# A two-layer diffusion trunk: second layer's output projection by token tiles, begun inside attention, with shared SBUF places and single PSUM banks

## Chip, cores and metric

One core of one Trainium2 chip runs the whole program. The metric is device time in microseconds of one execution, as the median of several runs. All arithmetic is 32-bit. TensorE (PE) multiplies; VectorE (DVE), ScalarE (ACT) and GpSimd (POOL) do the rest; SyncE (SP) issues most transfers, POOL's queue a few.

## The reference, cut to what matters

Two layers over 1024 latent tokens and 256 context tokens of width 1024. The first layer (grouped attention beside a gated scan, then a convolutional FFN) isn't touched. The second layer reads both and returns the latent tokens alone:

```python
def odd_mixer(h_lat, h_ctx, w_qkv, w_out, rpb, with_ctx_out):
    ...
    # per grid row: 8 x 16 neighbourhood plus all context keys in one softmax, 16 heads of 64
    o = lax.map(row_block, (jnp.arange(rows), q.transpose(1, 0, 2, 3, 4)))
    y_lat = o.transpose(1, 0, 2, 3, 4).reshape(B_, L, C_W) @ w_out
```

After the mixer: y is RMS-normed, multiplied by a gate, and added to the residual x2, which gives x3. Then x3 is RMS-normed, scaled and shifted, and goes through the FFN:

```python
def conv_ffn(h, w_up, conv_w, conv_b, w_down):
    u = h @ w_up
    u = lax.conv_general_dilated(u, conv_w[:, None, :], ...) + conv_b
    a, g = jnp.split(u, 2, axis=-1)
    return (jax.nn.silu(g) * a) @ w_down
```

with another gated residual behind it.

## The kernel before

**Exact products.** A 32-bit operand is split into a high part (a rounding copy, called `hi`, `h` or `..h`) and a low part (a subtraction). A product is three matmuls: high by high, high by low, low by high (L115 is the one line that records them all). A split costs one copy on ACT and one subtraction, on DVE or POOL.

**Stages of the second layer.** `odd_values` (L1766 on) norms x2, transposes it into `xh`, `xl` (channels by tokens, one tile of 40 KB per partition each) and projects the values, which go to DRAM (`vcd`). `odd_attention` computes the rest in one loop. `odd_out` is a stage of its own. `last` runs the FFN, `ffn(1, ...)`.

**Attention.** `project()` is a generator that yields after every three matmuls of the query and key projection; the loop over 128 jobs (16 heads, 8 query tiles) calls it through `step`, 46 times ahead and then two or three times per iteration. An iteration holds the scores of job i on PE, their minimum and bias on DVE (L2003), the exponential of job i-1 on ACT (L2009), the transposes of job i-3 with a copy on ACT and a subtraction on DVE (L2034, L2035), the values of job i-5, and the division of job i-1, a `tensor_scalar` on POOL over 640 columns (L2015). `finish` adds the halves of a head's output and stores them to DRAM (`ocd`, by pairs of heads, tokens grouped by 8-column strips). Projected queries and keys live in a ring of four places (`c_qa`, `c_qb`, `c_k`). Projection uses two PSUM banks (`g_ps`), transposes three, scores two, values one. The generator runs dry at job 110; the last 17 jobs and the drain run without it.

**Output projection.** `odd_out` loads `ocd` by halves of the tokens (two halves of 512, `a_oT`), splits it (L2209, L2210), and `out_proj` loads and splits the weights for each half of the columns and of the tokens anew (`granule`, L133, L135). For four token tiles at a time `y_half` squares and copies a PSUM bank out (L312, L313); `y_finish` loads x2 (L331), applies rstd and gate (L322), adds (L325) and stores x3 to DRAM (L326).

**FFN.** `ffn_norm` loads all rows of x3, norms each in SBUF (L1121 square, `rstd` with a power on POOL at L123, L1125 scale), transposes in groups of four tiles (L1145), applies scale and shift (L1157) and forms sums for a product scheme of seven half-size products instead of eight: operands `B11`, `B21` (first 512 tokens), `T1` to `T4`, `B22`, each split. `sums()` yields between these. `ffn_up` runs 22 feature tiles of 128 channels; `first(j)`, the product of A11 and B11, stands ahead of its tile. For j = 0 the loop draws `sums()` between products, and `add(u2, ...)`, which frees a bank for the S3 by T3 product, stands behind the T3 sums. `ffn_down` is behind the last tile.

**Order.** Within these stages `in_order` fixes the order of PE, ACT, DVE and POOL to the order of the program text; each engine's queue is served in order. SP's transfers are placed by the scheduler and then also issued in order, each behind the wait of the one ahead of it. A tile with one buffer is written again only when its last reader is done, and a pool that opens on memory of a closed pool waits tile by tile.

Of the kernel before, what the change touches and what calls it, by code (L numbers as in the profile page):

```python
# [20 lines left out]
P = 128  # L21
# [21 lines left out]
BLOCKS = ((0, 512), (512, 512), (1024, 256))  # L43

# [17 lines left out]
class Trunk:  # L62
# [54 lines left out]
    def rstd(self, ms, n, p=P):  # L117

        nc = self.nc
        e = self.small.tile([P, 16], F32, name="rs_e")  # L120
        r = self.small.tile([P, 16], F32, name="rs_r")
        nc.vector.tensor_scalar(e[:p, :n], ms, EPS, None, op0=OP.add)  # L122
        nc.gpsimd.tensor_tensor(out=r[:p, :n], in0=e[:p, :n], in1=self.mhalf[:p, :n], op=OP.pow)  # L123
        return r[:p, :n]

    def granule(self, src, a, b, lo="pool"):
# [9 lines left out]
        return hi, lo_t  # L136

# [204 lines left out]
    def qk_norm_rope(self, ps, nh, t, w, sp, dup):  # L342
# [7 lines left out]
        ms = self.small.tile([P, 16], F32, name="qk_ms")  # L350
# [850 lines left out]

    def ffn_up(self, l, src, ctx, x_src, x_dst, hp, pp, tp, es, beside):
# [58 lines left out]
        def first_out(j):  # L1261
            if j < FK:
                st["p1"] = half("f_p1")
                nc.scalar.copy(st["p1"], st["G", j][:, :512])
# [25 lines left out]
        with self.in_order(*self.compute), ExitStack() as loads:  # L1290
# [18 lines left out]
            sp = self.pool(es, f"fu{l}", 2)  # L1309
            cw = sp.tile([P, 48, 4], F32, name="cw", bufs=1)[:, 0:44, :]  # L1310
            nc.sync.dma_start(cw, a["convT"][l])
# [6 lines left out]
            first_out(0)  # L1318

            down = iter(())  # L1320
            for j in range(FK):
# [11 lines left out]
                product(st["G", j][:, :512], ("A12",), "B21", False, True)  # L1333
# [16 lines left out]
                split(n, "A11")  # L1350
# [4 lines left out]
                product(Z, ("S1",), "T1", True, False)  # L1355
                if j == 0:
                    next(sums)
                u2 = st["u2"] = half("f_u2")
                add(u2, V[:, 512:], st["p1"])
# [26 lines left out]
                first(n)  # L1386
# [379 lines left out]
    def odd_values(self, nx, xh, xl, gp, tp, sp):  # L1766
# [22 lines left out]
        def modulate(n0, tiles, s):  # L1789
            n = P * len(tiles)  # L1790
            for k in range(KT):
                pt = tp.tile([P, 512], F32, name="n_pt", tag="tp")
                for i, t in enumerate(tiles):
# [3 lines left out]
                nc.vector.tensor_copy(xh[:, k, n0:n0 + n], t[:, :n])  # L1797
                nc.vector.tensor_tensor(out=xl[:, k, n0:n0 + n], in0=t[:, :n], in1=xh[:, k, n0:n0 + n].bitcast(F32),
                                        op=OP.subtract)
# [13 lines left out]
        def products(tiles):  # L1813

            for c in range(2):
                for t in tiles:
                    ps = gp.tile([P, 512], F32, name="g_ps")
                    for k in range(KT):
                        wh, wl = (w[:, 512 * (k % 2):512 * (k % 2) + 512] for w in W[4 * c + k // 2])
                        xhk, xlk = xh[:, k, t * P:(t + 1) * P], xl[:, k, t * P:(t + 1) * P]  # L1820
# [58 lines left out]
    def odd_attention(self, xh, xl, gp, tp, pp, sp):  # L1879
# [9 lines left out]
        for i in range(4):  # L1889
            q1 = sp.tile([P, SEQ], F32R, name=f"c_qa{i}", bufs=1)  # L1890
            q2 = sp.tile([P, SEQ], F32R, name=f"c_qb{i}", bufs=1)
            kk = sp.tile([P, NTOK], F32R, name=f"c_k{i}", bufs=1)
            nc.gpsimd.memset(q2[64:128].bitcast(F32), 0.0)
            ring.append((q1, q2, kk))
# [30 lines left out]
        def evacuate(c, j, n0, n, ps, s):  # L1925

            q1, q2, kk = ring[(2 * c + s) % 4]
# [6 lines left out]
            else:  # L1934
                nc.scalar.copy(kk[0:64, cs], ps[r, :n])
                nc.vector.tensor_tensor(out=kk[64:128, cs], in0=ps[r, :n], in1=kk[0:64, cs].bitcast(F32), op=OP.subtract)

        def project():
# [3 lines left out]
            for c in range(KT):  # L1942
                for j, blocks in ((0, BLOCKS[:2]), (1, (BLOCKS[0], BLOCKS[2], BLOCKS[1]))):
                    for n0, n in blocks:
                        ps = gp.tile([P, 512], F32, name="g_ps")
                        for k in range(KT):
                            m = 4 * c + 2 * j + k // 4
                            wh, wl = (w[:, (k % 4) * P:(k % 4) * P + P] for w in wts[m])
                            xhk, xlk = xh[:, k, n0:n0 + n], xl[:, k, n0:n0 + n]
# [11 lines left out]
            yield KT  # L1961

# [12 lines left out]
        def value_load(h, ts):  # L1975
            for t in ts:
                v = sp.tile([P, 2, P], F32R, name="c_v", bufs=8)
# [6 lines left out]
        def scores(h, b, ql):  # L1984
            g = 2 * b + ql
            q1, q2, kk = ring[h % 4]
# [10 lines left out]
            for o, k0, w in parts:  # L1997
                for i, q in enumerate((q1, q2)):
                    self.mm(ps[:, o:o + w], q[:, g * P:(g + 1) * P], kk[:, k0:k0 + w], i == 0, i == 1)
# [55 lines left out]
        def finish(h, b, pv):  # L2055
            tu = sp.tile([P, 256], F32, name="c_o", bufs=1)
            o, t = tu[0:64], tu[64:128]
            nc.scalar.copy(t, pv[64:128, :256])
            nc.vector.tensor_tensor(out=o, in0=pv[0:64, :256], in1=t, op=OP.add)
            r = 64 * (h % 2)  # L2060
            nc.sync.dma_start(self.ocd[h // 2][r:r + 64, 256 * b:256 * b + 256], o)

        fill = project()
        at = 0
# [6 lines left out]
        with self.in_order(*self.compute):  # L2071
            load(0)
            load(1)
            for m in range(3):
                prepare(m)
            bias_load(0)
            value_load(0, (8, 0, 2))
            bias(0)
            step(46)
# [5 lines left out]
            for i in range(N + 6):  # L2085
                if i < N:
# [26 lines left out]
                step(1)  # L2113


    def run(self, stages=5):
        for f in (self.even_in, self.even_out, self.middle, self.odd_out, self.last)[:stages]:
# [55 lines left out]
    def odd_in(self, nx, early):  # L2173
        pool = self.pool
        with ExitStack() as es:
            hp = pool(es, "h1")
            xh = hp.tile([P, KT, NTOK], F32R, name="xh")
            xl = hp.tile([P, KT, NTOK], F32R, name="xl")
            with ExitStack() as e2:
                gp = pool(e2, "g_psum", 4, space=PSUM)  # L2180
                tp = pool(e2, "t_psum", 3, space=PSUM)
                sp = pool(e2, "n1", 2)
                self.weights(e2, 3, 8)
                self.odd_values(nx, xh, xl, gp, tp, sp)
            early.close()
            with ExitStack() as e2:
                sp = pool(e2, "na", 2)
                self.weights(e2, 2, 2)
                gp = pool(e2, "g_psum", 2, space=PSUM)
# [133 lines left out]
```

## Time and profile before

| quantity | value |
|---|---|
| median of three runs | 3415.87 us (3415.09 to 3416.26) |
| the profiled execution | 3415.23 us, its span 3413.3 us |
| granted TensorE clock, mean over the span | 0.957 |
| busy: PE, DVE, ACT, POOL | 91%, 60%, 44%, 45% |
| attention's loop with projection beside it | about 2165 to 2523 us |
| attention without it | 2523 to 2575 us |
| output projection | 2575 to 2683 us |
| norm of the FFN and its first feature tile | 2683 to 2773 us |
| FFN up, feature tiles at 19.05 us each | from there |

A slice of the page's second part is a fortieth of the span, and its digits are busy tenths. In a timeline row, the bracket at the end is how long the engine had stood idle and what released it. In a row of a group, the part behind the bar is the busy sum and the mean of one in ns, then the idle time ahead of it. In the chain of waits, a row is start, duration and what was waited for.

### The profile page before, as it was taken

How to read it: one execution, taken by the hardware profiler on the slowest of the kernel's cores; microseconds unless marked ns; L12 is line 12 of the kernel's file. 1: busy time of each engine (PE TensorE's matmuls, PEld its weight loads, DVE VectorE, ACT ScalarE, POOL GpSimd, SP SyncE). 2: the span in 40 equal slices, each digit the busy share in tenths (PEclk: the TensorE clock that was granted, in tenths of full speed). 3: DMA queues.
4: the chain of work that ended last, by engine and by line, in shares of the span. 5: the costliest groups of instructions: out<-in, count | busy, mean ns of one | idle time of the engine just before them, and what ended most of it. 6: DMA issues, size and time to landing. Idle time of an engine off the chain costs nothing.

```text
span 3413.3 us, 48746 instructions
## 1 busy us (share of the span) xinstructions
PE 3113.9 (91%) x18364; PEld 2567.7 (75%) x18364; DVE 2059.1 (60%) x3413; ACT 1487.1 (44%) x2619; POOL 1524.3 (45%) x1147
## 2 busy tenths in 40 slices
PE   5899998869998699999999989999997679999997
PEld 2776776658887488888878768898986468888785
DVE  3625666657775754545477863576775565555778
ACT  3223222256664543434344442566664344343443
POOL 1310111187774466666610111677771167777201
PEclk7999999979999799999999999999998799999998
DMA  7533333221112212212285772222216412222856
GB/s 233 161 100 130 129 119 115 101 90 38 50 44 73 95 68 68 71 63 73 75 299 194 255 237 110 69 61 65 63 45 186 139 53 90 75 91 75 272 186 214
DMA packets 203947, 399.24 MB, mean 117 GB/s; under 512 B 23216, under 2 KB 85168, under 8 KB 203712
## 3 DMA queue, kind: packets, MB, share of 16 engines
q1 hardware_dynamic: 194656, 364.15, 32.7%
q0 software_dynamic: 9056, 31.99, 2.4%
q8 instruction: 144, 2.36, 0.3%
q14 instruction: 91, 0.75, 0.1%
HBM read 322.11 MB, written 74.34 MB: 116 GB/s over the span
## 4 chain that ended last, share of the span: by engine, by line
PE 74%; DVE 10%; DMA 4%; ACT 4%; issue 4%; POOL 2%; SPq 1%; POOLq 0%; ACTq 0%; DVEq 0%
PE g_ps L115 20%; PE u_g L115 13%; PE d_ps L115 10%; PE u_v L115 10%; PE u_pc L115 4%; PE a_pv L115 2%; PE c_pv L115 2%; PE c_s L115 2%; PE a_pt L930 2%; PE c_pt L2032 2%; PE mod_ps L115 1%; DVE a_pl L932 1%; PE a_s L115 1%; ACT a_ph L931 1%; DMA y_x<-x2d 1%
## 5 line engine op out<-in xcount | busy, mean ns | idle before, releaser
L123 POOL TENSOR_TENSOR rs_r<-rs_e,mhalf 128x1 f32<-128x1 f32 (+3 forms) x106 | 81.1, 765 | 1006.7 <-DVE rs_e L122 1006.5
L115 PE MATMUL d_ps<-d_Bh,d_Ah 128*128 128x512 f32 x704 | 276.9, 393 | 9.5 <-ACT d_Bh L1460 9.4
L115 PE MATMUL g_ps<-xh,w_hi 128*128 128x512 f32 (+1 forms) x704 | 276.3, 392 | 5.9 <-ACT w_hi L544 5.9
L115 PE MATMUL d_ps<-d_Bl,d_Ah 128*128 128x512 f32 x704 | 277.7, 394 | 4.0 <-DVE d_Bl L1461 3.1
L115 PE MATMUL d_ps<-d_Bh,d_Al 128*128 128x512 f32 x704 | 276.8, 393 | 2.0 <-DVE d_Al L1461 1.9
L910 POOL TENSOR_SCALAR a_p<-a_p,rl 128x1280 f32<-128x1280 f32 (+1 forms) x80 | 240.3, 3008 | 72.7 <-DVE rl L909 58.6
L2015 POOL TENSOR_SCALAR c_p<-c_p,rl 128x640 f32<-128x640 f32 (+1 forms) x128 | 231.1, 1807 | 85.3 <-DVE rl L2014 61.7
L115 PE MATMUL g_ps<-xh,w_lo 128*128 128x512 f32 (+1 forms) x704 | 256.1, 364 | 1.6 <-DVE w_lo L545 1.2
L115 PE MATMUL g_ps<-xl,w_hi 128*128 128x512 f32 (+1 forms) x704 | 256.7, 365 | 0.0
L1242 DVE TENSOR_TENSOR f_u<-u_v,f_p 128x512 f32<-128x512 f32 x88 | 60.5, 688 | 185.1 <-PE u_v L115 185.1
L932 DVE TENSOR_TENSOR a_pl<-a_pt,a_ph 128x512 fp32r<-128x512 f32 (+1 forms) x200 | 118.7, 603 | 85.8 <-ACT a_ph L931 85.6
L115 PEld LDWEIGHTS g_ps<-xh,w_hi 128*128 128x128 f32 x704 | 134.3, 191 | 44.8 <-issue 27.6
L115 PEld LDWEIGHTS d_ps<-d_Bh,d_Ah 128*128 128x128 f32 x704 | 133.6, 190 | 39.6 <-ACT d_Bh L1460 10.8
L1228 POOL TENSOR_TENSOR w_S4l<-w_s,w_S4h 128x512 fp32r<-128x512 f32 x44 | 57.2, 1301 | 232.0 <-ACT w_S4h L1227 232.0
L115 PEld LDWEIGHTS d_ps<-d_Bl,d_Ah 128*128 128x128 f32 x704 | 133.5, 190 | 36.1 <-DVE d_Bl L1461 8.0
L115 PEld LDWEIGHTS d_ps<-d_Bh,d_Al 128*128 128x128 f32 x704 | 133.5, 190 | 30.9 <-DVE d_Al L1461 3.3
L115 PE MATMUL g_ps<-w_hi,xh 128*128 128x512 f32 (+1 forms) x400 | 154.2, 385 | 2.7 <-ACT w_hi L479 1.5
L931 ACT CAST a_ph<-a_pt 128x512 fp32r<-128x512 f32 (+1 forms) x200 | 103.0, 519 | 121.3 <-PE a_pt L930 121.3
L115 PE MATMUL g_ps<-w_lo,xh 128*128 128x512 f32 (+1 forms) x400 | 149.9, 375 | 3.5 <-DVE w_lo L1785 2.8
L115 PEld LDWEIGHTS g_ps<-xh,w_lo 128*128 128x128 f32 x704 | 133.7, 190 | 24.6 <-DVE w_lo L545 1.7
L115 PE MATMUL g_ps<-w_hi,xl 128*128 128x512 f32 (+1 forms) x400 | 150.1, 375 | 0.2 <-DVE xl L280 0.2
L2035 DVE TENSOR_TENSOR c_pl<-c_pt,c_ph 128x256 fp32r<-128x256 f32 (+1 forms) x256 | 113.1, 471 | 50.1 <-ACT c_ph L2034 48.8
(468 smaller groups left out, 9727.0 us busy)
## 6 DMA issues: line engine op xcount, KB each, us to landing
m_raw<-in_w_mod SPq DMA_DIRECT2D x96, 512.0 KB
w_raw<-in_w_up SPq DMA_DIRECT2D x88, 512.0 KB
d_rawA<-actd SPq DMA_DIRECT2D x77, 512.0 KB
d_rawB<-in_w_down SPq DMA_DIRECT2D x74, 512.0 KB
actd<-f_t SPq DMA_DIRECT2D x22, 640.0 KB
d_t<-in_w_down SPq DMA_DIRECT2D x22, 512.0 KB
actd<-f_t SPq DMA_DIRECT2D x22, 512.0 KB
d_s<-actd SPq DMA_DIRECT2D x20, 512.0 KB
```

The costliest lines, as they stand in the source:

```text
L115: return self.nc.tensor.matmul(out, lhsT, rhs, start=start, stop=stop, skip_group_check=True, **k)
L123: nc.gpsimd.tensor_tensor(out=r[:p, :n], in0=e[:p, :n], in1=self.mhalf[:p, :n], op=OP.pow)
L910: nc.gpsimd.tensor_scalar(Pt[:, :nk], Pt[:, :nk], rl, None, op0=OP.mult)
L930: nc.tensor.transpose(pt[:, m, qt * P:(qt + 1) * P], Pt[:, kts[j + m] * P:(kts[j + m] + 1) * P], self.ident)
L931: nc.scalar.copy(ph[:, j:j + n], pt[:, :n])
L932: nc.vector.tensor_tensor(out=pl[:, j:j + n], in0=pt[:, :n], in1=ph[:, j:j + n].bitcast(F32), op=OP.subtract)
L1228: nc.gpsimd.tensor_tensor(out=lo, in0=part(j, name), in1=hi.bitcast(F32), op=OP.subtract)
L1242: nc.vector.tensor_tensor(out=out, in0=x, in1=y, op=OP.add)
L2015: nc.gpsimd.tensor_scalar(Pt[:, :n], Pt[:, :n], rl, None, op0=OP.mult)
L2032: nc.tensor.transpose(pt[:, j, :], Pt[:, (src + j) * P:(src + j + 1) * P], self.ident)
L2035: nc.vector.tensor_tensor(out=vap(pl, o, dims), in0=pt[:, :cnt], in1=vap(ph, o, dims).bitcast(F32), op=OP.subtract)
```

## The change

`odd_out`, `middle` and `last` go; `second` holds the whole second layer. Its parts:

- Pools `hx` and `xc` stay open from the values to the FFN. Named places of 4 KB per partition (`OPND`, `RING`, `n_t22`, `xc..`) are used in turn for x, value weights, the ring of queries and keys, output weights, attention output and FFN operands. The context part of x and of the keys has tiles of its own. PSUM places are single banks by name.
- `odd_out_ahead` is appended to the generator `project()`: it loads and splits `odd_w_out` once, in 16 halves, into the places of x; from job 112 it loads seven pairs of heads of `ocd` one after the other into one place, splits the first 512 tokens, back in natural order, and multiplies token tiles 0 and 1 by the first 512 columns for seven of eight channel blocks. The output of the last two heads stays in SBUF (`oL`).
- `odd_out_norm` does the rest by token tiles: 114 steps of three products. A tile's chain (square, rstd, gate, residual, store of x3, square, rstd, scale into `xs`) is spread over the steps of the next tile. The other 512 tokens of `ocd` are loaded again and split in steps 2 to 16; the eight transposing groups of the first four tiles stand in steps 64 to 99.
- `second_front` then runs first FFN products beside the last tile's chain, the groups of the other four tiles, and goes on as before.
- For both layers, `add(u2, ...)` stands ahead of the sums of T3 at j = 0. Some small buffers drop from 8 to 4.

```diff
+OPND = [f"x_T{i}{j}{x}" for i in (1, 2, 3) for j in "01" for x in "hl"] + ["x_T40h", "x_T41h", "x_B220l", "x_B221l"]
+RING = [f"x_B{i}{j}{x}" for i in ("11", "21") for j in "01" for x in "hl"] + ["x_T40l", "x_T41l", "x_B220h", "x_B221h"]
...
-        e = self.small.tile([P, 16], F32, name="rs_e")
+        e = self.small.tile([P, 16], F32, name="rs_e", bufs=4)
...
+    def odd_out_norm(self, xs, first_half, op, load, early):
...
+        def post(i):
+            xs[i] = place(i)
+            for h in range(2):
+                nc.vector.scalar_tensor_tensor(out=xs[i][:, halves[h]], in0=ps[i, h], scalar=r[i], in1=gate[:, halves[h]],
+                                               op0=OP.mult, op1=OP.mult)
+        def add(i):
+            for h, x in enumerate(xa[i]):
+                nc.vector.tensor_tensor(out=x, in0=xs[i][:, halves[h]], in1=x, op=OP.add)
+                nc.gpsimd.dma_start(self.x3d[i * P:(i + 1) * P, halves[h]], x)
...
+        def chain(i):
...
+            yield square(ps[i, 1], ms1[i], 1)
+            yield rstd(ms1)
+            yield post(i)
+            yield add(i)
+            yield squares(i)
+            yield rstd(ms2)
+            yield
+            yield scale(i)
+            if i + 2 < 8:
+                yield load_x(i + 2)
+        def steps():
+            seq = [(0, 0, KT - 1), (1, 0, KT - 1)]
+            seq += [(i, 1, k) for i in range(2) for k in range(KT)]
+            seq += [(i, h, k) for i in range(2, 8) for h in range(2) for k in range(KT)]
+            chains, waits, groups = [], [], list(range(KT))
+            for n, (i, h, k) in enumerate(seq):
+                if (i, h) not in ps:
+                    ps[i, h] = self.banks2[2 * h + i if i < 2 else 2 * (i % 2) + h]
+                self.out_step(i, h, k, ps[i, h])
...
+                if n % 2 == 0 and 2 <= n < 2 + 2 * KT:
+                    c = (n - 2) // 2
+                    self.o_split(raws[c] if c < KT - 1 else self.oL, c, 1)
+                    load_o(c + 3)
...
+                if n >= 64 and (n - 64) % 5 == 0 and groups:
+                    first_half(groups.pop(0))
...
+        load_x(0)
+        load_x(1)
+        nc.sync.dma_start(gate, self.gated[1, 0, 0].partition_broadcast(P))
+        for c in range(3):
+            load_o(c)
+        self.o_split(self.oL, KT - 1, 0)
...
+        def second_front():
...
+            for _ in norm:
+                pass
+            load(1, 0)
+            next(tail)
+            self.ge.close()
+            pp, tp = (self.pool(es, n, 1, space=PSUM) for n in ("u_psum", "t_psum"))
+            first(0)
+            first_out(0, self.wp.tile([P, 512], F32, name="f_p1", tag="w_A21h", bufs=1))
+            next(tail)
+            product(st["G", 0][:, :512], ("A12",), "B21", False, True)
+            split(1, "A11")
+            first(1)
+            for _ in tail:
+                pass
...
+            for i, _ in enumerate(second_half):
...
-                if j == 0:
-                    next(sums)
                 u2 = st["u2"] = half("f_u2")
                 add(u2, V[:, 512:], st["p1"])
+                if j == 0:
+                    next(sums)
...
-            hi, lo = (self.wp.tile([P, 1024], F32R, name="w_" + x, bufs=8) for x in ("hi", "lo"))
+            if m < 6:
+                hi, lo = (self.tile2(t, "w_" + x, F32R) for t, x in zip(RING[2 * m:2 * m + 2], ("hi", "lo")))
...
+            yield from self.odd_out_ahead(at)
...
+    def odd_out_ahead(self, at):
...
+        def w_split(m):
+            k, h = halves[m]
+            if h == 0:
+                W[k] = [self.tile2(OPND[2 * k + i], "w_" + x, F32R) for i, x in enumerate(("hi", "lo"))]
+            hi, lo = (w[:, 512 * h:512 * h + 512] for w in W[k])
+            raw = raws.pop(m)
+            nc.scalar.copy(hi, raw)
+            nc.vector.tensor_tensor(out=lo, in0=raw, in1=hi.bitcast(F32), op=OP.subtract)
+            w_load(m + 2)
+        def o_load(c):
+            raws["o"] = self.tile2(RING[4], "o_raw")
+            nc.sync.dma_start(raws["o"], self.ocd[c])
+        w_load(0)
+        w_load(1)
+        for m in range(2):
+            w_split(m)
+            yield
+        while at["job"] < 112:
+            yield
+        o_load(0)
+        w_split(2)
+        yield
+        for k in range(6):
+            if k + 3 < KT:
+                w_split(k + 3)
+                yield
+            self.o_split(raws["o"], k, 0)
+            if k < 5:
+                o_load(k + 1)
+            yield
+            for i in range(2):
+                self.out_step(i, 0, k, self.banks2[i])
+                yield
+        for m in range(KT, 2 * KT):
+            w_split(m)
+            if m == KT + 3:
+                o_load(6)
+            yield
...
+    def o_split(self, raw, k, half):
...
+        src = vap(raw, 64 * half, ((8, 8), (P, 8), (1, 8)))
...
+        nc.scalar.copy(v(hi), src)
+        nc.vector.tensor_tensor(out=v(lo), in0=src, in1=v(hi.bitcast(F32)), op=OP.subtract)
+    def out_step(self, i, h, k, ps):
+        half, t = divmod(i, 4)
+        (xh, xl), (wh, wl) = self.oX[half, k], self.oW[k]
+        x, w = slice(P * t, P * t + P), slice(512 * h, 512 * h + 512)
+        self.mm(ps, xh[:, x], wh[:, w], k == 0, False)
+        self.mm(ps, xh[:, x], wl[:, w], False, False)
+        self.mm(ps, xl[:, x], wh[:, w], False, k == KT - 1)
```

More of the change, by code (lines that the diff above doesn't have):

```diff
@@ L1349, in ffn_up @@
                 total(n, "S2", "S1", OP.subtract, "A11")
[L1350 removed]
+                if j or l == 0:
+                    split(n, "A11")
                 if ctx:
@@ L1944, in project @@
                     for n0, n in blocks:
-                        ps = gp.tile([P, 512], F32, name="g_ps")
+                        turn[0] += 1
+                        ps = self.banks2[turn[0] % 2]
                         for k in range(KT):
@@ L2174, in odd_in @@
         pool = self.pool
[L2175 to L2189, printed above, removed]
-                tp = pool(e2, "t_psum", 3, space=PSUM)
-                pp = pool(e2, "na_psum", 1, space=PSUM)
-                self.odd_attention(xh, xl, gp, tp, pp, sp)
@@ L2194, in odd_out @@
[L2194 to L2213 removed]
+        self.odd_x_tiles()
@@ L2215, in ffn @@
+        with ExitStack() as e2:
+            gp = pool(e2, "g_psum", 4, space=PSUM)
+            tp = pool(e2, "t_psum", 3, space=PSUM)
+            sp = pool(e2, "n1", 2)
+            self.weights(e2, 3, 8)
+            self.odd_values(nx, gp, tp, sp)
+        early.close()
     def ffn(self, l, src, blocks, x_src, x_dst, stay, beside=None):
```

342 lines of the change are left out of this document (278 added, 64 removed).

## The prediction

> **What bounds the kernel now.** I read the page first, then busy time by stage, the chain of waits from the end of the neighbourhood attention to the second FFN, and the timelines of the engines around its joints. The page says that TensorE is busy for most of the span:
>
> ```profile
> PE   5899998869998699999999989999997679999997
> PEclk7999999979999799999999999999998799999998
> ```
>
> The weak place this change touches is the 7, 6, 7 of slices 31 to 33 (85.3 us each). Windows over it (columns: window and width in us, busy us and instructions of PE, weight loads, DVE, ACT, POOL, then granted clock, DMA share, GB/s):
>
> ```profile
> 2527.00:2565.00 38.00, 34.47 (x236) 30.67 (x234) 31.81 (x93) 29.61 (x77) 32.23 (x19) 0.96 0.18 45
> 2575.00:2684.00 109.00, 93.95 (x384) 74.85 (x384) 57.70 (x75) 36.64 (x64) 7.35 (x13) 0.91 0.60 184
> 2684.00:2773.00 89.00, 42.96 (x162) 31.95 (x163) 61.38 (x79) 40.64 (x68) 37.45 (x32) 0.69 0.30 107
> 2800.00:3100.00 300.00, 300.00 (x1322) 247.87 (x1322) 156.19 (x158) 119.44 (x172) 234.49 (x176) 1.00 0.23 81
> ```
>
> These are the end of attention without projection work beside it (17 iterations; DVE, ACT and POOL all near full), the output projection, the norm and first feature tile of the FFN, and the FFN's steady state. In the last, TensorE never idles, so whatever time is won ahead of 2800 us arrives at the end one for one; nothing behind absorbs it. The joints, from the timelines of PE, DVE and ACT:
>
> ```profile
> 2530.20 0.69 DVE L2003 CUSTOM_DVE_ANT_0 c_p<-c_s,c_be 128x512 f32<-128x512 f32 x1 [0.97 <-PE c_s L115]
> 2563.72 0.82 DVE L2003 CUSTOM_DVE_ANT_0 c_p<-c_s,c_bi 128x640 f32<-128x640 f32 x1
> 2574.58 0.42 DVE L2059 TENSOR_TENSOR c_o<-c_pv,c_o 64x256 f32<-64x256 f32 x1 [2.43 <-ACT c_o L2058]
> 2585.18 1.22 PE L115 MATMUL g_ps<-w_hi,a_oh 128*128 128x512 f32 x2 [11.35 <-ACT w_hi L133]
> 2682.76 0.39 PE L115 MATMUL g_ps<-w_hi,a_ol 128*128 128x512 f32 x1
> 2703.19 0.48 PE L1145 MATMUL n_pv<-ident,n_x 128*128 128x128 f32 x1 [20.04 <-DVE rs_e L122]
> 2755.75 0.76 PE L115 MATMUL u_v<-x_T30h,w_S3h 128*128 128x512 f32 x1 [10.97 <-DVE f_u L1242]
> 2772.57 0.50 PE L115 MATMUL u_g<-x_B210h,w_A12h 128*128 128x512 f32 x1 [1.34 <-ACT f_p L1264]
> ```
>
> The first two rows are jobs 112 and 127: 33.5 us for 15 iterations, 2.23 us each. Attention ends at 2575.0. The projection then waits 11.35 us for its first weights and ends at 2683.0: 108.0 us. Then come 20.04 us without a product, and the FFN's second feature tile starts at 2772.57: 89.6 us. The chain of waits names what fills the holes:
>
> ```profile
> 2577.11 5.68 DMA a_oT<-ocd
> 2584.59 5.77 DMA w_raw<-in_odd_w_out
> 2659.32 3.64 DMA w_raw<-in_odd_w_out
> 2684.54 4.91 DMA y_x<-x2d
> 2691.06 4.61 DMA x3d<-y
> 2695.86 3.43 DMA n_x<-x3d
> ```
>
> All of these are transfers that start when their result is already needed: attention output, output weights, residual, and the round trip of x3d through DRAM (4.61 + 3.43).
>
> **The change, part by part.** Prices:
>
> ```profile
> 2809.55 8.16 PE u_g L115 x36
> 2049.32 0.44 PE n_pt L1794 x4
> L2210 DVE TENSOR_TENSOR a_ol<-a_oT,a_oh 128x512 fp32r<-128x512 f32 x16 | 10.6, 689 | 9.2 <-ACT a_oh L2209 9.2
> L2209 ACT CAST a_oh<-a_oT 128x512 fp32r<-128x512 f32 x16 | 9.7, 617 | 9.9 <-DMA a_oT<-ocd 9.8
> L2015 POOL TENSOR_SCALAR c_p<-c_p,rl 128x640 f32<-128x640 f32 (+1 forms) x17 | 30.7, 1811 | 6.5 <-DVE rl L2014 2.6 <-ACT c_p L2009 2.5 <-PE c_pt L2032 1.0
> ```
>
> A 128x512 product costs 8.16/36 = 0.227 us, a transpose 0.11.
>
> *A. Work put into attention's tail.* After the last projection of queries and keys (job 110) the generator goes on with 16 weight halves (ACT cast, DVE subtraction), seven splits of attention output (the same pair) and 14 steps of three products. From job 112 that is 35 yields, five per two iterations, so 14 iterations. TensorE gets 42 x 0.227 = 9.5 us, ACT 23 x 0.62 = 14.2 us; both have room in 14 longer iterations. DVE gets 23 subtractions of 0.69 = 15.9 us, while it has (38.00 - 31.81)/17 = 0.36 us free per iteration, 5.1 us in 14. So at least +10.8 us. But these subtractions read two SBUF tensors, which by the code no DVE instruction of attention's loop does (there the low parts of weights are made on POOL), and POOL runs its 1.81 us divide. What such a meeting costs is seen in the FFN's front:
>
> ```profile
> 2749.91 1.75 DVE L1187 TENSOR_TENSOR x_t<-n_t,x_t 128x512 f32<-128x512 f32 x1
> 2752.94 0.69 DVE L1187 TENSOR_TENSOR x_t<-n_t,x_t 128x512 f32<-128x512 f32 x1
> 2749.39 1.71 POOL L1228 TENSOR_TENSOR w_A11l<-w_raw,w_A11h 128x512 fp32r<-128x512 f32 x1
> ```
>
> The same subtraction takes 1.75 us against a POOL instruction that started before it and 0.69 without one. At 1.75 each, 23 cost 40.3, +35.2 us after the free time. I take a chance meeting: with iterations stretched to some 3.7 us, POOL's 1.9 us per iteration fills half; the mean rest of a divide is 0.9 us; so 0.69 + 0.46 = 1.15 us, 26.5 - 5.1 = **+21 us** (bounds +11 and +35). The loads of the split's one raw place (512 KB, 5.77 us) are covered by two such iterations, 7.4 us; uncovered they are the slow rival below. Behind a late cast on ACT stands the exponential of the next job, and for that DVE, POOL and PE wait in turn.
>
> The Trainium skill bears on this (SBUF — State Buffer, section "Who interferes with whom"): a VectorE instruction with two SBUF inputs contends with a GpSimd instruction that reads SBUF, exclusively, and whichever issued later is blocked for the other's whole length. The two L1187 rows agree with it. By that rule taken every time, the sum would be the +35 rather than the +21; by the lone L2210 row it would be +11.
>
> *B. The projection by token tiles.* Its 384 products become 342 behind attention (77.5 us), with 32 transposes of the next norm between them (3.5 us). Weights are resident and split, so the weight waits go. Before the first product come the last cast and subtraction, 0.62 + 0.69 and hand-offs: 1.5 us. Each tile's chain (square, rstd, gate, residual, square, rstd, scale) runs while the next tile's 16 steps (10.9 us) are multiplied:
>
> ```profile
> L312 ACT ACTIVATE yjunk<-g_ps 128x512 bf16<-128x512 f32 x16 | 9.5, 596 | 51.1 <-PE g_ps L115 51.1
> L322 DVE SCALAR_TENSOR_TENSOR y<-y,rs_r,gate 128x1024 f32<-128x1024 f32 x8 | 10.3, 1285 | 5.5 <-POOL rs_r L123 5.5
> L325 DVE TENSOR_TENSOR y<-y,y_x 128x1024 f32<-128x1024 f32 x8 | 9.8, 1224 | 8.0 <-DMA y_x<-x2d 8.0
> L123 POOL TENSOR_TENSOR rs_r<-rs_e,mhalf 128x1 f32<-128x1 f32 x8 | 4.5, 560 | 80.0 <-DVE rs_e L122 79.8
> ```
>
> Four squares 2.4, two rstd with their DVE parts 1.9, gate 1.3, residual 1.2, scale 0.6: an estimate of 7.8 us with hand-offs, under 10.9. The banks leave 14 steps, for tile 0 only six. The tight place is the start: x2d (1 MB), gate (0.5) and three raw loads (1.5), then four more, with their casts in front of tile 0's square on ACT. At 184 GB/s (second window) 3 MB are 16 us, and tile 2 wants tile 0's bank 12.3 us after the start. If they start in attention's tail nothing is lost; if all start at its end, some 10 us. I take 4.5 us of stalls with a slow clock at the start (0 to 12). Sum 1.5 + 77.5 + 3.5 + 4.5 = 87.0 against 108.0: **-21 us**. The x3d stores stay on POOL's queue, idle here (7.35 of 109).
>
> *C. Norm and front of the FFN.* Store, reload and row norms go; half the groups are done. Behind the last product come 36 FFN products (8.2 us) that cover tile 7's chain (7.8); tile 1's A11 has one place, and its cast and subtraction end 1.9 us late: 10.1. Then eight groups and the T2 splits on ACT:
>
> ```profile
> 2731.99 0.78 ACT L1157 ACTIVATE n_t<-n_pv,mod,mod 128x512 f32<-128x512 f32 x1
> 2732.66 0.61 ACT L1104 CAST x_T21h<-x_t 128x512 fp32r<-128x512 f32 x1
> 2734.55 1.46 DVE L1107 TENSOR_TENSOR x_T21l<-x_t,x_T21h 128x512 fp32r<-128x512 f32 x2
> 2768.91 1.28 DVE L1107 TENSOR_TENSOR x_B221l<-n_t,x_B221h 128x512 fp32r<-128x512 f32 x2
> ```
>
> 8 x 0.78 + 6 x 0.61 (four T2 casts, two weight casts) and 1.4 for the last subtraction and hand-off: 11.3. From T2's end (2736.0) to 2772.57 DVE, with ACT and POOL, makes the other sums: 36.6 us, less 2.0 because POOL's A11 subtraction (1.71, above) no longer falls there: 34.6. Together 56.0 against 89.6: **-33.6 us** (bounds 50, no meetings; 64, tile 7's chain exposed).
>
> *At nothing:* u2's addition ahead of T3's sums removes the 10.97 us wait of PE, but DVE's sums are the path there (0 to -4.7 per layer, the twelve products after them). Weights of the values in shared places, the zeroing of the key halves split in two, fewer buffers for rstd: their readers are done long before the writers come; if not, one late 512 KB landing, 0 to +6. Score and key work is unchanged in count.
>
> **Sum:** +21 - 21 - 33.6 = -33.6 us against the profiled execution, 3415.23 us (span 3413.3): 3381.6, that is **3382**. That execution lies 0.6 us below the median, which I neglect.
>
> **Rivals.**
> 1. *The tail is free of meetings and loads come early* (divides are short of full time, SP's queue is nearly empty in the tail): A +11, B's stalls 0, C 53: 3382 - 10 - 4.5 - 3 = 3364. Against it: POOL's 85% in the first window.
> 2. *Every subtraction meets a divide*: A +35: 3396. For it: some follow the reciprocal that starts the divide.
> 3. *Slower: the single raw place.* In the tail each raw load is asked for only when the last subtraction has read, SP issues in order, and ACT stands at the cast with the exponential behind it. If the cover fails wholly, seven landings of 5.77 and two first weight halves of 3.64 are paid in full: +47.7, 3430. It decides from 4.8 us of waiting per load (33.6/7). Against it: the 7.4 us between splits, and a DMA share of 0.18 there.
> 4. *The change doesn't do what it says at the hand-over*: loads start only when attention frees its memory, ACT holds tile 0's bank, PE waits: 12 us more, 3394. For it: the new pools open on the memory that attention's pool gives up.
>
> **How the numbers follow.** Forecast 0.50 (its own range 3370 to 3392), rival 1 0.17, rival 2 0.16, rival 3 0.10, rival 4 0.07. Range: A's bounds (-10, +14), B's (-4.5, +7.5) and C's (-6, +8) seldom fall together; 3356 to 3406 leaves out rival 3 and the corners. What can be told from no change is about 0.2%, 6.8 us: faster below 3409 takes cases 1, 2, 4 and the forecast except corners, 0.86; same 0.04; slower 0.10.
>
> **What would show it.** A: jobs 112 to 126 at 3.7 us each, DVE the busiest, its new subtractions lasting 1.1 us on average (near 0.7: rival 1; 1.7: rival 2; ACT waiting on o_raw DMAs: rival 3). B: products at 0.227 us with gaps below 5 us in all from attention's end on (a gap ahead of tile 2: rival 4). C: second feature tile 56 us behind the last projection product, no x3d load on the chain. Wrong in direction if the tail grows by more than 55 us, or steady FFN tiles leave 19 us.

## The result, and the profile after

The changed kernel takes 3397.7 us (median of seven runs, 3394.2 to 3408.7) against 3415.9 us: a ratio of 0.9953, with a 95% interval of 0.9941 to 0.9966. It is faster, by 0.5%, where 1.0% was forecast: 16 us above the predicted time, with about half of the gain. The profiled execution took 3395.8 us (span 3393.9). Its slices, from the page:

```profile
PE   5899998869999599999999989999997989999997
PEclk8999999969999699999999989999999989999998
```

The 7, 6, 7 of slices 31 to 33 is gone; a 7 stands in slice 31. Windows (columns as before) over most of attention's end, the projection, the front of the FFN, and the steady FFN:

```profile
2536.00:2574.00 38.00, 30.28 (x171) 25.03 (x171) 27.62 (x68) 23.12 (x56) 20.57 (x12) 0.92 0.51 156
2608.00:2699.00 91.00, 85.80 (x378) 69.81 (x379) 40.55 (x88) 36.80 (x86) 18.78 (x30) 0.96 0.43 146
2699.00:2755.00 56.00, 38.59 (x128) 23.84 (x127) 42.49 (x50) 27.04 (x49) 30.02 (x23) 0.79 0.15 47
2800.00:3100.00 300.00, 300.00 (x1324) 248.11 (x1323) 156.25 (x158) 119.00 (x171) 234.52 (x176) 1.00 0.24 81
```

The first row is the surprise. Before, POOL and DVE were busy for 32 of 38 us there. Now work was added, and every engine is *less* busy: 27.6 us on DVE, 20.6 on POOL. Where work grows and all engines idle more, they must be waiting for each other or for a transfer; the experiments tell for which. The joints, from the timelines of DVE and PE:

```profile
2536.49 0.67 DVE L2296 CUSTOM_DVE_ANT_0 c_p<-c_s,c_be 128x512 f32<-128x512 f32 x1
2597.12 0.82 DVE L2296 CUSTOM_DVE_ANT_0 c_p<-c_s,c_bi 128x640 f32<-128x640 f32 x1
2608.62 0.51 PE L119 MATMUL g_ps<-w_hi,o_h 128*128 128x512 f32 x1 [1.56 <-ACT o_h L2496]
2625.40 0.80 PE L119 MATMUL g_ps<-w_hi,o_h 128*128 128x512 f32 x1 [3.95 <-DVE y L1330]
2698.18 0.39 PE L119 MATMUL u_g<-x_B110h,w_A11h 128*128 128x512 f32 x1
2754.59 0.44 PE L119 MATMUL u_g<-x_B210h,w_A12h 128*128 128x512 f32 x1
```

Jobs 112 and 127 are now 60.6 us apart (33.5 before). The projection starts 1.56 us after attention and ends at 2698.3; the second feature tile starts 56.2 us behind it. The span, cut at such events (first transpose of the values' stage, first score, jobs 112 and 127, last attention product, last projection product, second feature tile), in us:

```
                      before    after   change   predicted
ahead of the values   2008.8   2011.4    +2.5      0
values' stage          156.1    159.4    +3.3      0  (0 to +6)
attention to job 112   365.3    365.7    +0.4      0
jobs 112 to 127         33.5     60.6   +27.1    +21  (+11 to +35)
drain                   10.1      9.9    -0.2      0
projection             109.3     91.3   -18.0    -21
front of the FFN        89.4     56.2   -33.2    -33.6
rest                   640.8    639.3    -1.5      0
span                  3413.3   3393.9   -19.4    -33.6
```

### The profile page after: what moved, and what is told of

Its sections match the earlier page's. It is cut to its first block, busy times and chain, and to the rows that moved or that the text cites. A ratio compares the mean times of both kernels' runs of the same rounds, so it can differ in the third digit from the quotient of the medians.

```text
span 3393.9 us, 48741 instructions
## 1 busy us (share of the span) xinstructions
PE 3117.6 (92%) x18364; PEld 2565.9 (76%) x18364; DVE 2038.5 (60%) x3421; ACT 1485.7 (44%) x2643; POOL 1528.8 (45%) x1155
## 4 chain that ended last, share of the span: by engine, by line
PE 76%; DVE 10%; DMA 4%; ACT 4%; issue 3%; POOL 2%; SPq 1%; POOLq 0%; ACTq 0%; DVEq 0%
PE g_ps L119 21%; PE u_g L119 13%; PE d_ps L119 11%; PE u_v L119 10%; PE u_pc L119 4%; PE a_pv L119 2%; PE c_pv L119 2%; PE c_s L119 2%; PE a_pt L949 2%; PE c_pt L2325 2%; PE mod_ps L119 1%; DVE a_pl L951 1%; PE a_s L119 1%; PE o_ps L119 1%; ACT a_ph L950 1%
## 5 line engine op out<-in xcount | busy, mean ns | idle before, releaser
L929 POOL TENSOR_SCALAR a_p<-a_p,rl 128x1280 f32<-128x1280 f32 (+1 forms) x80 | 240.0, 3002 | 72.4 <-DVE rl L928 60.4
L119 PE MATMUL g_ps<-xh,w_hi 128*128 128x512 f32 (+1 forms) x640 | 257.3, 402 | 7.9 <-ACT w_hi L563 6.5
L119 PE MATMUL g_ps<-xh,w_lo 128*128 128x512 f32 (+1 forms) x640 | 238.2, 372 | 2.6 <-POOL w_lo L2208 1.4
L119 PE MATMUL g_ps<-xl,w_hi 128*128 128x512 f32 (+1 forms) x640 | 238.7, 373 | 0.0
L951 DVE TENSOR_TENSOR a_pl<-a_pt,a_ph 128x512 fp32r<-128x512 f32 (+1 forms) x200 | 118.8, 603 | 85.0 <-ACT a_ph L950 84.9
L119 PEld LDWEIGHTS g_ps<-xh,w_hi 128*128 128x128 f32 x640 | 122.3, 191 | 47.0 <-issue 27.5
L119 PEld LDWEIGHTS d_ps<-d_Bh,d_Al 128*128 128x128 f32 x704 | 133.5, 190 | 30.6 <-DVE d_Al L1740 3.3
L119 PE MATMUL g_ps<-w_hi,xh 128*128 128x512 f32 (+1 forms) x368 | 142.4, 387 | 2.8 <-ACT w_hi L498 1.6
L2327 ACT CAST c_ph<-c_pt 128x256 fp32r<-128x256 f32 (+1 forms) x256 | 99.0, 414 | 99.2 <-PE c_pt L2325 97.2
L119 PEld LDWEIGHTS g_ps<-xh,w_lo 128*128 128x128 f32 x640 | 121.7, 190 | 25.5 <-POOL w_lo L2208 1.8
L119 PE MATMUL g_ps<-w_lo,xh 128*128 128x512 f32 (+1 forms) x368 | 137.9, 375 | 2.7 <-DVE w_lo L2069 1.9
```

Of the source, the lines that this page charges most:

```text
L119: return self.nc.tensor.matmul(out, lhsT, rhs, start=start, stop=stop, skip_group_check=True, **k)
L929: nc.gpsimd.tensor_scalar(Pt[:, :nk], Pt[:, :nk], rl, None, op0=OP.mult)
L951: nc.vector.tensor_tensor(out=pl[:, j:j + n], in0=pt[:, :n], in1=ph[:, j:j + n].bitcast(F32), op=OP.subtract)
L2327: nc.scalar.copy(vap(ph, o, dims), pt[:, :cnt])
```

## The experiments

Each kernel differs from the changed one by the diff shown or the edit named. Ratios are against the kernel before, with their intervals; stages are from each kernel's profile, cut as above. Code ahead of the values' stage is the same in most of them, and that stage begins between 2008 and 2017 us: single profiles differ by up to 8 us there, so stages are compared rather than spans. In the five profiles in which the code of the tail (job 112 to 127) is as in the changed kernel it lasts 60.6 to 62.1 us; smaller differences say nothing.

**What the tail waits for.** The waits of ACT and of PE in the changed kernel, from 2536 to 2595 us (us in total, times, longest):

```profile
ACT c_ph L2327 <- PE c_pt L2325: 13.0, 10, 2.4
ACT w_hi L2441 <- DMA w_raw<-in_odd_w_out: 6.0, 6, 1.5
ACT o_h L2496 <- DMA o_raw<-ocd: 1.7, 3, 0.9
...
PE g_ps L119 <- ACT o_h L2496: 7.5, 6, 1.9
PE c_s L119 <- DVE nm L2296: 4.8, 2, 3.7
PE g_ps L119 <- DVE o_l L2497: 2.2, 4, 1.0
```

and the chain of waits holds a loop in the middle of the same stretch:

```profile
2550.72 3.42 DMA o_raw<-ocd
2554.17 0.63 ACT o_h L2496
2554.82 0.70 DVE o_l L2497
2555.54 4.31 DMA o_raw<-ocd
2559.87 0.63 ACT o_h L2496
2560.52 0.87 DVE o_l L2497
2561.41 4.28 DMA o_raw<-ocd
```

Landing, cast, subtraction, next landing: 4.8 to 5.9 us a round. The waits with a DMA's name are small (1.7 us for `o_raw`), yet these rounds are in the chain: an engine that works in order and comes late to its cast shows a short wait. There are three theories: the landings set the pace (L), DVE's added work does (D), or PE stands at products of a split that was made just before (P).

*More raw places.* `o_raw` gets a second place (one that a finished head's keys leave free), the weight halves eight instead of two:

```diff
-            raws["o"] = self.tile2(RING[4], "o_raw")
+            raws["o", c] = self.tile2((RING[4], RING[2])[c % 2], "o_raw")
-                raws[m] = self.wp.tile([P, 512], F32, name="w_raw", bufs=2)
+                raws[m] = self.wp.tile([P, 512], F32, name="w_raw", tag=tag, bufs=bufs)
-            w_load(m + 2)
+            w_load(m + 8)
```

> Edit: attention output gets two raw places in the tail instead of one (each load asked for two splits ahead), the output weights' halves eight raw places instead of two. Work and order of the engines stay. Theory L (landings: in the tail each raw load is asked for only after the subtraction that frees its place, and ACT, DVE and PE stand in order behind the cast): the stretch from job 112 to job 127 falls from 60.6 us by 8 to 15 us, to 46-53. Rival D (DVE work: 23 subtractions more than DVE has room for): no change, 58-62. Rival P (PE stands at products of a split that was made just before): at most 2 us less, 58-61. The time follows one for one.

Jobs 112 to 127: 54.2 us, 6.4 less; ratio 0.9948 (0.9933 to 0.9963). That is more than D and P allow, and a little less than the 8 us that L asked for at least. Both kinds of place were changed at once, so how the 6.4 us divide between attention output and weights is not known. ACT no longer waits for any DMA there, but PE still waits for the split:

```profile
PE g_ps L119 <- DVE o_l L2499: 4.3, 6, 1.6
PE g_ps L119 <- ACT o_h L2498: 2.9, 6, 0.6
```

*Products one block later,* with the places as they were:

```diff
             self.o_split(raws["o"], k, 0)
...
-            for i in range(2):
-                self.out_step(i, 0, k, self.banks2[i])
+            for i in range(2 if k else 0):
+                self.out_step(i, 0, k - 1, self.banks2[i])
```

> Edit: in the tail the products of a channel block stand behind the split of the next block instead of directly behind their own split; loads, places and counts stay. Rival P: PE's waits for the high part (7.5 us) and low part (2.2 us) of attention output go, job 112 to 127 falls from 60.6 to about 51. Theory L: the single raw place still sets the pace, 57-61. Rival D: no change, 59-62.

60.4 us, ratio 0.9962 (0.9952 to 0.9972): nothing, as L says. PE's 9.7 us of waits did go, and stood elsewhere at once, with ACT at the landing and PE's scores behind it:

```profile
PE c_s L119 <- DVE nm L2296: 11.0, 7, 4.1
PE g_ps L119 <- ACT o_h L2502: 0.9, 1, 0.9
...
ACT o_h L2502 <- DMA o_raw<-ocd: 11.1, 4, 5.0
```

So P alone falls; whether it is next in line, a later kernel had to show.

*Nothing ahead:* the generator waits for iteration 133 instead of 112.

```diff
-        while at["job"] < 112:
+        while at["job"] < 133:
```

> Edit: the work ahead (14 of 16 weight halves, seven splits of attention output, 14 steps of products) starts at the last iteration instead of at job 112, so that it stands behind attention. Both theories: job 112 to 127 falls back to 33.5 us (27 less). Theory L: behind attention the same loop of load, cast and subtraction runs nearly alone, six landings at about 5.7 us a round and the weights between them: 40-55 us more there, 13 to 28 us slower than the changed kernel in all. Rival D: behind attention DVE is nearly free, the 23 casts and subtractions and 14 steps take some 20-27 us, so the time stays within 7 us of the changed kernel.

Ratio 1.0009 (0.9999 to 1.0018), 20 us above the changed kernel (medians). The tail is back at 34.8, and the projection takes 134.0 instead of 91.3 us: +42.7, within L's range; D allowed 27. The waits of ACT behind attention:

```profile
ACT o_h L2496 <- DMA o_raw<-ocd: 17.5, 5, 4.3
ACT w_hi L2441 <- DMA w_raw<-in_odd_w_out: 13.1, 5, 4.1
```

ACT stands 30.6 us at landings there, with no attention left beside them. Beginning inside attention thus costs 25.8 us of tail and saves 42.7 us behind it.

**The stall in the projection.** PE waits 3.95 us ahead of tile 2 (row at 2625.40 above). DVE's `y` waits for tile 0's square, and ACT's timeline shows why that is late:

```profile
2614.85 0.62 ACT L2496 CAST o_h<-w_raw 128x512 fp32r<-128x512 f32 x1 [3.50 <-DMA w_raw<-ocd]
...
2619.70 0.62 ACT L2496 CAST o_h<-w_raw 128x512 fp32r<-128x512 f32 x1 [1.73 <-DMA w_raw<-ocd]
2620.23 0.59 ACT L1325 ACTIVATE junk<-o_ps 128x512 bf16<-128x512 f32 x1
2620.71 0.19 ACT L1325 ACTIVATION_READ_ACCUMULATOR junk<-o_ps 128x1 f32 x1
2622.30 0.62 ACT L2496 CAST o_h<-w_raw 128x512 fp32r<-128x512 f32 x1 [1.40 <-DMA w_raw<-ocd]
2623.66 0.62 ACT L2496 CAST o_h<-w_raw 128x512 fp32r<-128x512 f32 x1 [0.74 <-DMA w_raw<-ocd]
```

Square and rstd stand between casts of tokens that are not needed before step 50, each waiting for a reload. The edit moves those splits by 16 steps:

```diff
-                if n % 2 == 0 and 2 <= n < 2 + 2 * KT:
-                    c = (n - 2) // 2
+                if n % 2 == 0 and 18 <= n < 18 + 2 * KT:
+                    c = (n - 18) // 2
```

> Edit: the splits of the second 512 tokens (reloaded attention output) stand in steps 18 to 32 of the output projection instead of 2 to 16; they are needed at step 50. Theory A (ACT stands at casts whose loads land late, tile 0's square behind them, PE waits 4.6 us for tile 0's bank and then runs 12 products at the slow clock): both go, the stretch from the end of attention to the last projection product falls from 91.3 to about 84 us, the time by 7. Rival X (residual and gate land late, or the chain itself is too long): 89-91 us, at most 2 less.

The projection takes 86.0 us instead of 91.3, and of PE's waits only the first (1.6 us) is left. That is 5.3 of the expected 7 us: A holds, X doesn't. The stall is gone whole, but a slow clock now stands at the start of the projection. The first six microseconds behind attention, in the changed kernel and then in this one (columns as before, granted clock third from the end):

```profile
2607.00:2613.00 6.00, 4.44 (x19) 3.31 (x19) 1.11 (x2) 2.36 (x6) 0.00 (x0) 1.00 0.78 226
```
```profile
2614.00:2620.00 6.00, 4.44 (x11) 3.43 (x12) 1.11 (x2) 2.36 (x6) 0.00 (x0) 0.55 0.78 229
```

The first 24 products take 8.3 us instead of 5.9, which is most of what is missing. The time as a whole does not show the gain (ratio 0.9946, 0.9931 to 0.9961): in that profile the values' stage is 2.6 us longer and the tail 1.5, and the interval is 10 us wide.

**The three together,** more places, later products, later splits:

> Edit: the three of before together: more raw places in the tail, products of a block behind the split of the next, splits of the second 512 tokens in steps 18 to 32. Theory LP (two waits in a row on one path: first the landings; once they are early, TensorE's wait for the split made just before, 7.2 us with more raw places alone, becomes worth its length): job 112 to 127 goes from 54.2 us with more raw places alone to 46-49. Rival L (only the landings count): 53-56. Rival D (DVE's work is what is left): 52-55. In both, end of attention to the last projection product is 84-86 us.

3376.5 us, ratio 0.9885 (0.9869 to 0.9901): faster than both kernels. Tail 45.9, projection 84.9 us. Both waits were on one path, one hidden behind the other: alone their edits gave 6.4 and 0.3 us, together 14.7 (the later splits don't act there: 62.1 in their own run). The window from job 112 to 127:

```profile
2534.10:2580.00 45.90, 39.47 (x256) 33.68 (x255) 42.04 (x106) 37.20 (x89) 30.08 (x18) 1.00 0.37 120
```

DVE is busy for 42.0 of 45.9 us, so what is left looks like its work. The same window of the kernel before has it at 28.6 of 33.5:

```profile
2530.20:2563.70 33.50, 30.38 (x214) 26.78 (x212) 28.58 (x83) 26.64 (x68) 28.26 (x18) 0.99 0.17 44
```

*A slower pace* (from job 112 on two pieces per iteration, so that some fall in the drain; `step(i % 2 if i < 112 else 0)`):

> Edit: as the three together, and from job 112 on two pieces of the work ahead per iteration instead of two and three in turn, so that its last ones fall in the drain of attention, where the engines are less than full. Theory S (each iteration is made longer by what is put in it; the drain has room): from job 112 to the end of attention 2 to 5 us less than the three together. Rival: the pieces cost the same wherever they stand, within 1.5 us of the three together.

Tail and drain take 54.8 us against 55.8, ratio 0.9891 (0.9876 to 0.9905): the rival holds, the pieces cost the same in the drain.

*Eight subtractions on POOL* (second halves of the output weights):

> Edit: as the three together, but eight of the 23 subtractions in the tail (second halves of the output weights) on POOL instead of DVE. Theory D2 (with landings and waits gone DVE's work is what is left: it is busy for 42.0 of the 45.9 us): job 112 to 127 falls by 3 to 5.5 us (8 x 0.69) to 40.5-43. Rival C (POOL's divide, which the transposes wait for, stands behind the new subtractions, and the two engines get in each other's way when both read SBUF): 45-50.

47.0 us, ratio 0.9901 (0.9888 to 0.9915): no gain, as rival C has it. Its window and the timeline of POOL show DVE relieved, at 37.1 us, POOL at 39.3 instead of 30.1, and a divide between new subtractions:

```profile
2540.60:2587.70 47.10, 41.00 (x255) 35.67 (x253) 37.11 (x99) 37.18 (x89) 39.33 (x25) 0.94 0.38 117
```
```profile
2575.00 3.74 POOL L2443 TENSOR_TENSOR w_lo<-w_raw,w_hi 128x512 fp32r<-128x512 f32 x3
2578.73 1.87 POOL L2308 TENSOR_SCALAR c_p<-c_p,rl 128x640 f32<-128x640 f32 x1
```

PE's transposes wait 3.8 us for divides there, against 1.7 with the three together. So DVE's work is the likely rest of the tail, but taking some of it off DVE did not show it.

**The edits priced at nothing.** *u2's addition* moved back behind the sums:

```diff
+                if j == 0:
+                    next(sums)
                 add(u2, V[:, 512:], st["p1"])
-                if j == 0:
-                    next(sums)
```

> Edit: in both layers u2's addition stands behind the sums of T3 again at the first feature tile. If its move costs in the first layer: first FFN product to first product of the down projection goes from 565.5 us to about 564.2 there; in the second layer the end of the projection to the second feature tile stays within 1 us of 56.3 (my prediction: at nothing, 0 to 4.7 won by the move) or grows by up to 4.7. Rival: neither stretch changes by over 0.5 us.

No cost and no gain can be told: the front of the FFN is 56.2 us with either order. In the first layer, from the first FFN product to the first of the down projection, this run has 563.4 us; with the move it is 565.5 in one profile and 563.9 in another, so a difference of 1 us can't be told there.

*The values' stage* is 3.3 us longer, 2.8 to 6.3 in the profiles with its code unchanged. SP's timeline, before and then after:

```profile
2109.34 0.42 SPq L1885 DMA_DIRECT2D rmask<-in_rmask  x1
```
```profile
2137.14 3.97 SPq L2271 DMA_DIRECT2D c_v<-vcd  x8
2141.15 0.47 SPq L2169 DMA_DIRECT2D rmask<-in_rmask  x1
```

The mask went out at 2109.34, and now at 2141.15. Values now load into shared places that are free early, so the scheduler takes their loads up first; they wait for the values' stores, and masks and bias stand behind them on SP. POOL stands 4.05 us at `L2186` for the mask. That alone makes nothing late; what does is the wait behind it, for the bias, whose loads stand behind the masks on SP. The same addition on POOL, before and after:

```profile
2145.09 1.01 POOL L1971 TENSOR_TENSOR c_be<-rmask,c_e 128x384 f32<-128x384 f32 x1
```
```profile
2151.08 1.01 POOL L2261 TENSOR_TENSOR c_be<-rmask,c_e 128x384 f32<-128x384 f32 x1 [5.09 <-DMA c_e<-ed]
```

Counted from the start of the values' stage it is 3.5 us late, and POOL's low parts of the weights come behind it. Two edits put SP in the order of the text at the start of attention, as far as the first values and as far as the eighth job:

> Edit: the first transfers of attention on SP (masks, first weights, first bias, first values) are issued in the order of the text; nothing else. Theory Q (the new places of the values let SP take their loads up first; they wait for stores of the values, masks and bias stand behind them, POOL and then TensorE are late): first transpose of the values' stage to first score goes from 159.4 us to 156-157.5. Rival (single PSUM banks or the zeroing of the key halves makes the start late): 159 or more.

168.2 us, ratio 0.9979 (0.9967 to 0.9990).

> Edit: SP's transfers are issued in the order of the text from attention's masks to the eighth job, so that the loads of later values stand behind the masks too (in the try before, two loads of the next head's values stayed ahead and held everything, 168.2 us). Theory Q (loads of values, taken up early because their places are free early, hold SP until the values are stored; masks, bias and weights are late behind them): first transpose of the values' stage to first score 154.5-158 us against 159.4 to 162.4 without it and 156.1 in the kernel before. Rival (the memory of the masks comes free late, or the value stage itself is slower): 159 or more.

166.9 us, ratio 0.9977 (0.9964 to 0.9989). With the three together:

> Edit: the three together, and SP in the order of the text up to the eighth job. Theory Q: 3 to 5 us less than the three together, 3371 to 3374. Rival: no gain or a loss, 3376 to 3382.

165.5 us and 0.9911 (0.9897 to 0.9925), about 8 us slower than without it by the medians. All three miss what Q forecast, because the edits did not put the bias early: in the first, two loads of values from behind the ordered part stayed ahead and now held the weights too; in the others the third to fifth weight loads, which wait for a place, held the bias:

```profile
2104.72 48.71 SPq L2202 DMA_DIRECT2D w_raw<-in_w_qk  x5
2153.49 5.39 SPq L2258 DMA_DIRECT2D c_e<-ed  x16
```

The right edit puts only the values' loads of two heads behind the first bias load:

```diff
+            known = self.names()
             bias_load(0)
+            st["bias"] = self.sp_new(known)[-1].name
             value_load(0, (8, 0, 2))
...
+                if h < 2:
+                    self.sp_behind(known, st["bias"])
```

> Edit: the three together, and on SP only the loads of the first two heads' values (c_v, c_vc) are put behind the first bias load; masks and weights keep their places (in the two tries before, weights or values held the bias). Theory Q: masks and bias come early again, POOL is in time, first transpose of the values' stage to first score 156.5-158.5 us instead of 159.8 with the three together; what is left above 156.1 is the 1.8 us in which the first query product waits for a bank. Rival (the masks' memory comes free late in the new layout): 159 or more. The time: 3372-3376 by Q, 3376-3380 by the rival.

157.5 us, as expected, below the 158.9 to 162.4 of all nine profiles with that code unchanged, and the mask leaves early again:

```profile
2109.27 0.44 SPq L2183 DMA_DIRECT2D rmask<-in_rmask  x1
```

The time, 3375.2 us, ratio 0.9896 (0.9879 to 0.9912), cannot be told from the three's. What stays of the 3.3 us is 1.4 (157.5 - 156.1), as much as PE's wait for the copy of the last value tile, which is in this run's waits too, with the same 1.4 us; that it comes of the single banks was not tried. The row from the changed kernel:

```profile
PE g_ps L119 <- DVE cv_st L2093: 1.4, 1, 1.4
```

## Why the prediction was right and wrong

**Direction and most terms held.** The front of the FFN was forecast at 56.0 us and took 56.2, and its parts agree too: 10.1, 11.3 and 34.6 came out as 9.8 (products of tile 1's A11 end at 2708.2), 11.5 (last low part of T2 at 2719.7) and 34.9. There the time was a sum of chains that the old profile showed row by row. The projection was to become 21 us shorter and became 18.0 shorter, with the stall where it was named, ahead of tile 2, and for the named cause, casts in front of tile 0's square.

**The step that failed is in part A:** "The loads of the split's one raw place (512 KB, 5.77 us) are covered by two such iterations, 7.4 us". They landed faster (3.4 to 4.3 us) and were not covered all the same. Splits are four pieces apart, at five pieces per two iterations: that is 1.6 iterations and not two, 5.9 us at the 3.7 us that were themselves assumed. Of these the load gets only what lies between its request, behind a subtraction, and the next cast: 5.9 - 0.62 - 0.69 = 4.6 us, less than the 5.77 us given for it. The landings of the eight second weight halves, one per piece with two places, were not costed at all; 4.5 of ACT's 6.0 us are theirs. What the runs showed in place of the cover: a loop of 4.8 to 5.9 us a round and, behind it, PE at products of the split just made, together 14.7 us that go when both are taken away. So rival 3 was right about the place and wrong about its size, priced as all or nothing.

**The contention that carried the term hardly came.** The group rows of the tail:

```profile
L2442 DVE TENSOR_TENSOR w_lo<-w_raw,w_hi 128x512 fp32r<-128x512 f32 x14 | 10.6, 760 | 4.5 <-ACT w_hi L2441 4.4
L2497 DVE TENSOR_TENSOR o_l<-o_raw,o_h 128x512 fp32r<-128x512 f32 x7 | 5.5, 791 | 1.1 <-ACT o_h L2496 1.1
```

A subtraction lasted 0.77 us, not 1.15, and there are 14 + 7 = 21 of them, not 23: the first two weight halves are split ahead of job 112. Their 16.1 us, less the 5.1 us that were free, make 11.0, near the 12.4 that the tail costs with both waits gone (45.9 - 33.5). The +27.1 is these 12.4 plus 14.7 us of waits. The forecast of +21 had some 10 us too much of subtractions and nothing for the waits; that it came as near as 6 us is luck. The signature named for it (1.1 us, DVE the busiest) was absent: PE was busy for 45.6 and DVE for 43.5 of the 60.6 us, standing idle in turn.

**Sizes.** A was 6.1 us too small. B was 3.0 too small, mostly at the stall: it was sized 4.5 with its clock, and cost 4.6 us of waits and 2.5 of half clock (last section). The values' stage cost 3.3 of the 0 to 6 that was bounded, at a place not named: not a late landing of 512 KB, but the order of SP's queue. 2.5 us lie ahead of all of it, within the spread of that stretch, and 1.5 come back in the rest. 6.1 + 3.0 + 0.4 + 3.3 + 2.5 + 0.4 - 0.2 - 1.5 = 14.0 of the 14.2 us between 33.6 and 19.4, the rest is rounding. One bound doesn't fit its own working either: the three lower bounds together give 3361.5, so the range's 3356 lies below the corner that it was said to leave out.

## What to carry to other kernels

Work put into a stage with idle engines can cost its longest loop there, not only its sum of engine time: write down request, landing, cast, release for each raw place, and compare the round with the spacing of the pieces, counted in the code. In queues served in order, let a consumer stand one piece behind its producer, and keep casts that wait for transfers out of the way of a chain that is due earlier. Of two waits on one path, taking away one can show little or nothing; try both together. A new free place also moves transfers ahead in a queue; look at what then stands behind them.

## What the runs showed of the hardware

**A divide on POOL blocked DVE little.** The timelines of POOL and DVE after:

```profile
2533.01 1.88 POOL L2308 TENSOR_SCALAR c_p<-c_p,rl 128x640 f32<-128x640 f32 x1 [1.02 <-ACT w_hi L2441]
```
```profile
2533.29 1.06 DVE L2442 TENSOR_TENSOR w_lo<-w_raw,w_hi 128x512 fp32r<-128x512 f32 x1
```

The subtraction began within the divide and ended 0.54 us ahead of its end. By the timelines 12 of the change's 23 began within a divide: the seven that began in its first 0.5 us took 0.86 to 1.06 us, the five that began 0.98 us or more behind its start 0.69, as without one. Beside a POOL operation with two SBUF tensors one of that size took 1.75 us in the kernel before. The Trainium skill (SBUF — State Buffer, section "Who interferes with whom") has the later of a VectorE instruction with two SBUF inputs and a GpSimd instruction that reads SBUF blocked for the other's whole instruction; the rows above don't agree with that for a POOL operation with one tensor.

**Behind a wait of 3.95 us the clock cost 2.5 us more.** The window behind it in the changed kernel (columns as before):

```profile
2625.40:2630.60 5.20, 5.20 (x12) 4.13 (x13) 3.80 (x8) 2.36 (x6) 1.58 (x3) 0.50 0.27 101
```

Twelve products took 5.2 us, where 12 x 0.227 are 2.7. The Trainium skill (TensorE: Matmul & The Clock Gate, section "Part 1: The HAM clock gate") gives half speed after an idle window of about 3.4 us, until a busy one of that length; the trace agrees with the half, and its slow stretch was longer. With the later splits 13 products at the start of the projection ran at clock 0.50 behind a wait of 1.56 us; the same wait stands there in the changed kernel, with products at clock 1.00 behind it. So the length of the last wait alone does not tell the clock in these runs.
